# Turning attention and residual blocks by DMA instead of on TensorE, and the gate/up products in natural order of k

## The chip, the cores and the metric

One core of one Trainium2 chip runs the whole program. The metric is the device time of one execution in microseconds (us). The median of three runs of the kernel before is 2124.01 us.

## The reference, cut to what matters

A trunk of two pre-norm layers over a residual `h` of 256 positions by 2048 features, all in float32. Layer 0 mixes with sliding-window attention and an mLSTM, layer 1 with a forgetting attention (FoX) of 16 heads of 128. Each layer ends with a SwiGLU feed-forward of width 5632.

```python
for layer in range(DEPTH):
    xn = rms_norm(h, norm_mix[layer])
    mix = swa_mlstm_mixer(xn, ...) if layer % 2 == 0 else forgetting_attention_mixer(xn, ...)
    h = h + mix                                   # mix ends with "@ w_out"
    h = h + swiglu(rms_norm(h, norm_ffn[layer]), w_gate[layer], w_up[layer], w_down[layer])
return rms_norm(h, norm_final)

def forgetting_attention_mixer(xn, w_in, b_f, w_out):
    q, k, v, f = split_cols(xn @ w_in, FOX_SIZES)     # 16 heads of 128 for each of q, k, v
    s = q @ k.T * scale + c[:, None] - c[None, :]     # c: running sum of log sigmoid(f); causal
    return (softmax(s) @ v).reshape(B, S, FOX_MIX) @ w_out

def swiglu(xn, w_gate, w_up, w_down):
    return (silu(xn @ w_gate) * (xn @ w_up)) @ w_down
```

## The kernel before, in words

**A matrix product.** Every product with a weight matrix keeps float32 accuracy by splitting both factors into a rounded high part and a low rest, and adding three TensorE products (`hi*hi`, `hi*lo`, `lo*hi`). Weights come in chunks of 256 rows by 512 columns ("a k pair": two tiles of 128 rows). SyncE's DMA queue loads a chunk into `raw` (L105, 512 KB; four buffers in the pool `wr`), ScalarE casts it to `hi` (L161), VectorE subtracts to make `lo` (L162); `hi` and `lo` have six buffers each. The chunk is used by 12 matmuls of 512 columns, in `gemm` (L192 to L194) or in `pair_group` (through `three`, L402 to L404). The activations are the stationary operands and must have the features on the partitions: `xh`, `xl` hold the normed residual so turned and split, `mh`, `ml` the mixer's or the hidden result.

**Turning.** There are two ways to get a block turned. *On TensorE*: eight transposes of 128x128 through the identity into PSUM (L245 in `split_scaled` for the residual; L306 in `transpose_many`, followed by a VectorE copy at L307, for q and k). *By DMA*, in `split_turned`: ScalarE copies the block's float32 words apart into two planes of 16 bits (L272, two instructions), four `dma_start_transpose` on SyncE's queue turn the planes (L274), and later a function `join` puts the two halves of each word together again (L279, two ScalarE copies) and calls `split_scaled` on the result. `scrap` finds the two buffers for that. A block `n` of the residual is 512 features: k tiles 4n to 4n+3, so k pairs 2n and 2n+1.

**When a join runs.** `out_proj` and `ffn` put a join with a due step into a list (`later` or `todo`); `run_due` emits it right behind the chunk load of that step. In `gemm` the step is counted in chunks, in `pair_group` it is the position in the order of k pairs.

**The output projection** (`out_proj`) makes the four blocks of `h` in two halves, `n0` = 0 and 2. Blocks 0 and 1 are turned by DMA while the second half is computed; blocks 2 and 3 are turned on TensorE as soon as they are added.

**Gate and up** (`ffn` calls `pair_group` for each of 11 groups of 512 hidden features and each layer). Per group, eight k pairs of two matrices: the positions written `(0, pair)` in `ORDER` are plain (24 matmuls), those written `(1, pair)` are mixed (a Strassen-like form: 21 matmuls, but more VectorE operations, L440 to L443 and L295, and sums of the activations made by `sums_of`). Before, the mixed ones are pairs 2, 3 and 6 at positions 2, 4 and 6. The down projection uses the same function with its own orders `DOWN`, in which the mixed ones of a group of eight are pairs 1, 3 and 5 at positions 1, 3 and 5.

**FoX.** For each of four head groups `i`, q, k and v are projected in turn (16 k tiles each), q and k are scaled into a natural tile (L865 in `nat1`) and turned on TensorE into `qtf` and `ktf`, and the scores start after v (L316, L323).

**What sets the order.** The program is recorded as written; a scheduler then orders each engine's instructions ahead of time, and each engine and each DMA queue runs its own list strictly in order, held by semaphores. SyncE's list holds the chunk loads and the DMA transposes alike.

Of the kernel before, what the change touches and what calls it, by code (L numbers as in the profile page):

```python
# [7 lines left out]
F32 = mybir.dt.float32  # L8
# [24 lines left out]
OFF_QM, OFF_KM, OFF_VM, OFF_OM = 1536, 2048, 2560, 3584  # L33
CAP = 15.0
FILL = 24
ORDER = ((0, 0), (0, 1), (1, 2), (0, 4), (1, 3), (0, 5), (1, 6), (0, 7))
DOWN = {
    6: ((0, 0), (1, 1), (0, 2), (1, 3), (0, 4), (0, 5)),
    8: ((0, 0), (1, 1), (0, 2), (1, 3), (0, 4), (1, 5), (0, 6), (0, 7)),
}  # L40
MID = 6
MID_DOWN = 5
LATER = (6, 10)
LATER_DOWN = (5, 6)
RAWS = 4
PARTS = (0, 3, 7, 11)
# [9 lines left out]
def trunk(  # L56
# [153 lines left out]
    def square_sum(key, n):  # L210
        if n == 0:
            sums[key] = sm.tile([P, NT, 4], F32, tag="ss", name="ss")
        for t in range(NT):
            junk = sm.tile([P, NB], BF16, tag="junk", name="junk", bufs=1)
            nc.scalar.activation(
                junk, h[:, t, n * NB : (n + 1) * NB], AF.Square, accum_out=sums[key][:, t, n : n + 1]
            )
# [50 lines left out]
    def split_turned(idx, n, flat, turned, extra=None):  # L268
        planes = flat.bitcast(U16).rearrange("p (b t n) -> p b t n", b=2, t=NT)
        hu = h[:, :, n * NB : (n + 1) * NB].bitcast(U16).rearrange("p t (n b) -> p t n b", b=2)  # L270
        for b in range(2):
            nc.scalar.copy(planes[:, b, :, :], hu[:, :, :, b])  # L272
            for t in range(NT):
                nc.sync.dma_start_transpose(turned[:, b, :, t, :], planes[:, b, t, :])  # L274

        def join():
            ju = flat.bitcast(U16).rearrange("p (n b) -> p n b", b=2)
            for b in range(2):
                nc.scalar.copy(ju[:, :, b], turned[:, b, :, :, :].rearrange("p k t q -> p (k t q)"))  # L279
            split_scaled(idx, n, extra, flat.rearrange("p (k s) -> p k s", k=4))  # L280

        return join

    def scrap(fp, n):
        if n == 0:
            box = fp.tile([P, 4, NB], F32, tag="c", name="box", bufs=1)
            halves = box[:, 0:2, :], box[:, 2:4, :]
        else:
            halves = [fp.tile([P, CK, NB], F32, tag="raw", name="box", bufs=RAWS) for _ in range(2)]
        flat, turned = (a.rearrange("p a n -> p (a n)") for a in halves)  # L290
        return flat, turned.bitcast(U16).rearrange("p (b k t q) -> p b k t q", b=2, t=NT, q=P)
# [92 lines left out]
            split_plain(mh[:, ks, :], ml[:, ks, :], po)  # L384

    def out_proj(w, idx, key, extra):
        last = KT - 4
        for n0 in (0, 2):
            accs = [new_acc() for _ in range(2)]
            for i in range(2):  # L390
                gemm(accs[i], m_of, w, (n0 + i) * NB, NB, 0, last, KT, step=6 * i)
            for i in range(2):
                gemm(accs[i], m_of, w, (n0 + i) * NB, NB, last, KT, KT, step=6)
                add_out(accs[i], n0 + i)
                if n0 == 0:
                    later.append((LATER[i], split_turned(idx, i, *scrap(extra[2], i), extra)))
                else:
                    split_scaled(idx, n0 + i, extra)
                square_sum(key, n0 + i)

    def three(o, ah, al, hi, lo, start, stop):
        nc.tensor.matmul(o, ah, hi, start=start, stop=False)  # L402
# [67 lines left out]
        nc.vector.tensor_tensor(out=c[:, 3, :], in0=prods[1], in1=c[:, 1, :], op=ALU.add)  # L470
        return plain, c

    def ffn(layer, fp, sx, sd, key, idx_next=None, key_next=None, finish=None):
        r = rstd(key)

        def sums_x(pair):
# [3 lines left out]
        for g0, g1 in zip(PARTS, PARTS[1:]):  # L480
            end = g1 == PARTS[-1]
            nk = 4 * (g1 - g0)
            order = DOWN[nk // 2]
            todo = []
            for g in range(g0, g1):
                par = (g1 - 1 - g) % 2
                plain, c = pair_group(
# [99 lines left out]
    def close_layer(layer, w_out, idx, key, **rest):  # L587
        with tc.tile_pool(name=f"fp{layer}", bufs=2) as fp:
            nx = len(mixed_of(ORDER))
            nd = max(len(mixed_of(o)) for o in DOWN.values())  # L590
            sx = [fp.tile([P, nx, 4, P], F32R, name=f"sx{i}", bufs=1) for i in range(2)]
            sd = [fp.tile([P, nd, 4, P], F32R, name=f"sd{i}", bufs=1) for i in range(2)]
            out_proj(w_out, idx, key, (*sx, fp))
            ffn(layer, fp, sx, sd, key, **rest)


    acc0 = new_acc()
# [263 lines left out]
    with tc.tile_pool(name="od", bufs=1) as od:  # L861
        def nat1(acc, n, name, bufs=1):
            t_ = od.tile([P, NT, n], F32, tag=name, name=name, bufs=bufs)
            for t in range(NT):
                nc.scalar.mul(t_[:, t, :], acc[t][:, 0:n], r1[:, t : t + 1])  # L865
            return t_

        VT = 2 * FD
        c_v = 2 * FOX_H * FD
        acc = project(wi1, c_v + 14 * FD, VT + FOX_H)  # L870
        fg = od.tile([P, NT, FOX_H], F32, name="fg")
        for t in range(NT):
            nc.vector.scalar_tensor_tensor(
                out=fg[:, t, :],
                in0=acc[t][:, VT : VT + FOX_H],
                scalar=r1[:, t : t + 1],
                in1=bias_f,
                op0=ALU.mult,
                op1=ALU.add,
            )  # L880
        vtail = nat1(acc, VT, "vtail")
        nl = od.tile([P, NT, FOX_H], F32, name="nl")
        nc.scalar.activation(nl, fg, AF.Abs)
        nc.scalar.activation(nl, nl, AF.Exp, scale=-1.0)
        nc.scalar.activation(nl, nl, AF.Ln, bias=1.0)
        nc.vector.scalar_tensor_tensor(out=nl, in0=fg, scalar=0.0, in1=nl, op0=ALU.min, op1=ALU.subtract)
        nc.vector.tensor_scalar(nl, nl, -1.0, None, op0=ALU.mult)
        pc = pm.tile([P, NB], F32, tag="pm", name="pcf")
        nc.tensor.matmul(pc[:, 0:FOX_H], upper, nl[:, 0, :], start=True, stop=True)
        nc.tensor.matmul(pc[:, FOX_H : 2 * FOX_H], ones, nl[:, 0, :], start=True, stop=False)  # L890
        nc.tensor.matmul(pc[:, FOX_H : 2 * FOX_H], upper, nl[:, 1, :], start=False, stop=True)
        negc = od.tile([P, NT, FOX_H], F32, name="negc")
        nc.vector.tensor_copy(negc.rearrange("p t h -> p (t h)"), pc[:, 0 : 2 * FOX_H])
        pr = pm.tile([P, NB], F32, tag="pm", name="prf")
        nc.tensor.matmul(pr[0:FOX_H, 0:P], nl[:, 0, :], upper, start=True, stop=True)
        nc.tensor.matmul(pr[0:FOX_H, P:S], nl[:, 0, :], ones, start=True, stop=False)
        nc.tensor.matmul(pr[0:FOX_H, P:S], nl[:, 1, :], upper, start=False, stop=True)
        negct = od.tile([FOX_H, S], F32, name="negct")
        nc.vector.tensor_copy(negct, pr[0:FOX_H, 0:S])
        scratch = dp.tile([FOX_H, S], F32, name="scratch")  # L900
        nc.gpsimd.dma_start(scratch, negct)
        cb1 = od.tile([P, FOX_H, S], F32, name="cb1")
        nc.gpsimd.dma_start(cb1, scratch.partition_broadcast(P))
        cb0 = od.tile([P, FOX_H, P], F32, name="cb0")
        for dst, src in ((cb0, cb1[:, :, 0:P]), (cb1[:, :, P:S], cb1[:, :, P:S])):
            nc.gpsimd.affine_select(
                out=dst, in_=src, pattern=[[0, FOX_H], [-1, P]], compare_op=ALU.is_ge, fill=NEG, base=0, channel_multiplier=1
            )

        for i in range(4):  # L910
            qt = od.tile([P, 4, S], F32, tag="qt", name="qtf")
            kt = od.tile([P, 4, S], F32, tag="kt", name="ktf")
            for off, dst in ((0, qt), (FOX_H * FD, kt)):
                n_ = nat1(project(wi1, off + i * NB, NB), NB, "qk")
                for g in range(0, 4, 2):
                    transpose_many(
                        dst[:, g : g + 2, :].rearrange("p g (t q) -> p (g t) q", q=P),
                        [n_[:, t, (g + u) * FD : (g + u + 1) * FD] for u in range(2) for t in range(NT)],
                    )
            vn = nat1(project(wi1, c_v + i * NB, NB if i < 3 else VT), NB if i < 3 else VT, "vn")  # L920

            def v_of(j, b, i=i, vn=vn):
                if i == 3 and j >= 2:
                    return vtail[:, b, (j - 2) * FD : (j - 1) * FD]
                return vn[:, b, j * FD : (j + 1) * FD]

            attention(
                od,
                lambda j, b, qt=qt: qt[:, j, b * P : (b + 1) * P],
                lambda j, kt=kt: kt[:, j, :],  # L930
                v_of,
                FD,
                FD**-0.5,
                cb0[:, 4 * i : 4 * i + 4, :],
                cb1[:, 4 * i : 4 * i + 4, :],
                4 * i,
                negc=negc[:, :, 4 * i : 4 * i + 4],
            )
# [76 lines left out]
```

## Time and profile before

| | |
|---|---|
| median of three runs | 2124.01 us (2122.88 to 2124.37) |
| the profiled execution's own time | 2122.88 us |
| its span from first to last instruction | 2121.2 us, so 1.7 us lie around it |
| TensorE busy (PE) | 2105.2 us, 99% of the span |
| VectorE (DVE), ScalarE (ACT), GpSimd (POOL) busy | 1719.5, 1277.0, 39.6 us |
| granted TensorE clock | 0.999 |
| DMA engines, mean | 199 GB/s, 421.48 MB moved |

PE is the matmul, PEld its weight load; SPq is SyncE's DMA queue. A matmul's listed duration (389 ns) includes its time in the pipeline; the next one starts some 0.227 us later, and it is the distance from start to start that counts.

### The profile page before, as it was taken

To read this page: it belongs to the slowest core of one execution; us is meant where nothing else is said; L and a number is where in the kernel's file an instruction comes from. 1 tells how busy PE (TensorE), PEld (TensorE's weight loads), DVE (VectorE), ACT (ScalarE), POOL (GpSimd) and SP (SyncE) were. 2 spreads that over 40 slices of the span, in tenths; PEclk is the share of its full clock that TensorE was granted. 3 is DMA by queue.
4 is the path that set the end of the run, shared out by engine and by line. 5 is a ranking of instruction groups with operands and counts; after the bars stand their busy time and mean duration, and the time that the engine had idled before them with its cause. 6 is when DMAs were issued, how large, how long until landed. Compare 5 with 4: busy or idle time off the path is not lost.

```text
span 2121.2 us, 26858 instructions
## 1 busy us (share of the span) xinstructions
PE 2105.2 (99%) x9699; PEld 1747.9 (82%) x9699; DVE 1719.5 (81%) x2212; ACT 1277.0 (60%) x1612; POOL 39.6 (2%) x61
## 2 busy tenths in 40 slices
PE   8999999999999999999999999999999999999998
PEld 7888888888888888888888888888888888888886
DVE  6665558999999999999855554579999999989994
ACT  6565457765567656766645544576755667556763
POOL 2110000000000000000000000000000000000000
PEclk9999999999999999999999999999999999999999
DMA  8454547666567666666575564676656666656754
GB/s 267 145 157 149 170 149 268 209 203 215 191 211 225 215 207 216 209 202 215 163 231 168 169 179 140 194 237 210 215 196 208 218 196 224 225 188 212 224 182 147
DMA packets 267942, 421.48 MB, mean 199 GB/s; under 512 B 67136, under 2 KB 75424, under 8 KB 267552
## 3 DMA queue, kind: packets, MB, share of 16 engines
q1 hardware_dynamic: 267136, 416.02, 61.6%
q0 software_dynamic: 624, 3.72, 0.5%
q8 instruction: 76, 1.25, 0.2%
q14 instruction: 58, 0.48, 0.1%
q10 hardware_dynamic: 48, 0.02, 0.0%
HBM read 404.48 MB, written 2.11 MB: 192 GB/s over the span
## 4 chain that ended last, share of the span: by engine, by line
PE 98%; ACT 1%; issue 0%; DMA 0%; DVE 0%; DVEq 0%; POOLq 0%; POOL 0%; ACTq 0%
PE acc L402 17%; PE acc L403 17%; PE acc L404 17%; PE acc L192 10%; PE acc L193 10%; PE acc L194 10%; PE prod L402 4%; PE prod L403 4%; PE prod L404 4%; PE p L323 1%; PE ptm L306 1%; PE po L374 1%; PE pt L245 0%; PE pp L366 0%; PE p L316 0%
## 5 line engine op out<-in xcount | busy, mean ns | idle before, releaser
L161 ACT CAST hi<-raw 128x1024 fp32r<-128x1024 f32 (+2 forms) x681 | 692.5, 1032 | 598.5 <-PE acc L404 307.6
L162 DVE TENSOR_TENSOR lo<-raw,hi 128x1024 fp32r<-128x1024 f32 (+2 forms) x681 | 807.3, 1201 | 259.5 <-ACT hi L161 256.2
L403 PE MATMUL acc<-lo,xh 128*128 128x512 f32 x946 | 368.1, 389 | 0.0
L402 PE MATMUL acc<-hi,xh 128*128 128x512 f32 x946 | 367.4, 389 | 0.0
L404 PE MATMUL acc<-hi,xl 128*128 128x512 f32 x946 | 366.8, 389 | 0.0
L192 PE MATMUL acc<-hi,xh 128*128 128x512 f32 (+3 forms) x736 | 275.8, 377 | 0.8 <-ACT hi L161 0.8
L193 PE MATMUL acc<-lo,xh 128*128 128x512 f32 (+3 forms) x736 | 275.8, 375 | 0.0
L194 PE MATMUL acc<-hi,xl 128*128 128x512 f32 (+3 forms) x736 | 275.5, 376 | 0.0
L404 PEld LDWEIGHTS acc<-hi,xl 128*128 128x128 f32 x946 | 177.6, 188 | 36.9
L402 PEld LDWEIGHTS acc<-hi,xh 128*128 128x128 f32 x946 | 177.5, 188 | 36.8
L403 PEld LDWEIGHTS acc<-lo,xh 128*128 128x128 f32 x946 | 177.6, 188 | 36.7
L403 PE MATMUL acc<-lo,mh 128*128 128x512 f32 x437 | 170.0, 389 | 0.0
L402 PE MATMUL acc<-hi,mh 128*128 128x512 f32 x437 | 168.1, 389 | 0.0
L404 PE MATMUL acc<-hi,ml 128*128 128x512 f32 x437 | 167.9, 389 | 0.0
L192 PEld LDWEIGHTS acc<-hi,xh 128*128 128x128 f32 x736 | 138.7, 189 | 24.8 <-ACT hi L161 1.2
L193 PEld LDWEIGHTS acc<-lo,xh 128*128 128x128 f32 x736 | 139.0, 189 | 24.2 <-issue 0.9
L194 PEld LDWEIGHTS acc<-hi,xl 128*128 128x128 f32 x736 | 138.8, 189 | 24.5 <-issue 0.8
L295 DVE TENSOR_TENSOR lt<-raw,ht 128x1024 fp32r<-128x1024 f32 x95 | 115.9, 1220 | 15.6 <-ACT ht L294 15.6
L294 ACT CAST ht<-raw 128x1024 fp32r<-128x1024 f32 x95 | 99.8, 1050 | 45.7 <-PE acc L404 26.9
L192 PE MATMUL acc<-hi,mh 128*128 128x512 f32 x320 | 125.3, 392 | 1.2 <-ACT mh L294 1.2
L193 PE MATMUL acc<-lo,mh 128*128 128x512 f32 x320 | 125.3, 392 | 0.0
L194 PE MATMUL acc<-hi,ml 128*128 128x512 f32 x320 | 123.9, 390 | 0.0
(313 smaller groups left out, 3120.4 us busy)
## 6 DMA issues: line engine op xcount, KB each, us to landing
raw<-in_w_gate_dram SPq DMA_DIRECT2D x176, 512.0 KB, 4.4
raw<-in_w_up_dram SPq DMA_DIRECT2D x176, 512.0 KB, 4.7
raw<-in_w_down_dram SPq DMA_DIRECT2D x176, 512.0 KB, 4.8
raw<-in_w_in_odd_dram SPq DMA_DIRECT2D x88, 512.0 KB, 3.9
raw<-in_w_in_even_dram SPq DMA_DIRECT2D x64, 512.0 KB, 4.1
raw<-in_w_out_even_dram SPq DMA_DIRECT2D x32, 512.0 KB, 3.6
raw<-in_w_out_odd_dram SPq DMA_DIRECT2D x32, 512.0 KB, 4.1
raw<-in_w_in_odd_dram SPq DMA_DIRECT2D x8, 272.0 KB, 2.8
```

The costliest lines, as they stand in the source:

```text
L161: latest[0] = nc.scalar.copy(hi[:, :, 0:n], raw[:, :, 0:n])
L162: nc.vector.tensor_tensor(out=lo[:, :, 0:n], in0=raw[:, :, 0:n], in1=hi[:, :, 0:n].bitcast(F32), op=ALU.subtract)
L192: nc.tensor.matmul(o, ah[:, ts], hi, start=(k == 0), stop=False)
L193: nc.tensor.matmul(o, ah[:, ts], lo, start=False, stop=False)
L194: nc.tensor.matmul(o, al[:, ts], hi, start=False, stop=(k == k_all - 1))
L294: nc.scalar.copy(dst_h, src)
L295: nc.vector.tensor_tensor(out=dst_l, in0=src, in1=dst_h.bitcast(F32), op=ALU.subtract)
L306: nc.tensor.transpose(pt[:, i, :], s_, ident)
L323: nc.tensor.matmul(p1[:, jj, :], q_of(j, 1), k_of(j), start=True, stop=True)
L402: nc.tensor.matmul(o, ah, hi, start=start, stop=False)
L403: nc.tensor.matmul(o, ah, lo, start=False, stop=False)
L404: nc.tensor.matmul(o, al, hi, start=False, stop=stop)
```

## The change

`ORDER` now has the mixed pairs 1, 3 and 5 at positions 1, 3 and 5, with all pairs in natural order. Blocks 2 and 3 of both output projections are turned by DMA too; their joins are handed to the first gate/up group of the layer with due positions 3 and 5. `scrap` gives block 2 the buffer of `c`, block 3 that of the sums `sd0`, `sd1` (which are not used before the down projection). In FoX, q and k of head groups 0, 1 and 2 are turned by DMA in a new function `turn`, joined six chunks into the next projection; head group 3 stays on TensorE.

```diff
-ORDER = ((0, 0), (0, 1), (1, 2), (0, 4), (1, 3), (0, 5), (1, 6), (0, 7))
+ORDER = ((0, 0), (1, 1), (0, 2), (1, 3), (0, 4), (1, 5), (0, 6), (0, 7))
-LATER = (6, 10)
+AHEAD = 6
+LATER = (6, 10, 3, 5)
...
     def scrap(fp, n):
-        if n == 0:
+        if n % 2 == 0:
             box = fp.tile([P, 4, NB], F32, tag="c", name="box", bufs=1)
             halves = box[:, 0:2, :], box[:, 2:4, :]
+        elif n == 3:
+            halves = [fp.tile([P, 3, NB], F32, tag=f"sd{i}", name="box", bufs=1)[:, 0:CK, :] for i in range(2)]
         else:
             halves = [fp.tile([P, CK, NB], F32, tag="raw", name="box", bufs=RAWS) for _ in range(2)]
...
     def out_proj(w, idx, key, extra):
-        last = KT - 4
+        last, rest = KT - 4, []
...
-                if n0 == 0:
-                    later.append((LATER[i], split_turned(idx, i, *scrap(extra[2], i), extra)))
-                else:
-                    split_scaled(idx, n0 + i, extra)
+                (later if n0 == 0 else rest).append(
+                    (LATER[n0 + i], split_turned(idx, n0 + i, *scrap(extra[2], n0 + i), extra))
+                )
                 square_sum(key, n0 + i)
+        return rest
...
-    def ffn(layer, fp, sx, sd, key, idx_next=None, key_next=None, finish=None):
+    def ffn(layer, fp, sx, sd, key, todo, idx_next=None, key_next=None, finish=None):
...
-            todo = []
...
-            out_proj(w_out, idx, key, (*sx, fp))
-            ffn(layer, fp, sx, sd, key, **rest)
+            todo = out_proj(w_out, idx, key, (*sx, fp))
+            sd = [fp.tile([P, nd, 4, P], F32R, tag=f"sd{i}", name=f"sd{i}", bufs=1) for i in range(2)]
+            ffn(layer, fp, sx, sd, key, todo, **rest)
...
+        def turn(src, dst):
+            planes = od.tile([P, 2, NT, NB], U16, tag="planes", name="planes")
+            turned = od.tile([P, 2, 4, NT, P], U16, tag="turned", name="turned")
+            su = src.bitcast(U16).rearrange("p t (n b) -> p t n b", b=2)
+            for b in range(2):
+                nc.scalar.copy(planes[:, b, :, :], su[:, :, :, b])
+                for t in range(NT):
+                    nc.sync.dma_start_transpose(turned[:, b, :, t, :], planes[:, b, t, :])
+            def join():
+                du = dst.rearrange("p k s -> p (k s)").bitcast(U16).rearrange("p (n b) -> p n b", b=2)
+                for b in range(2):
+                    nc.scalar.copy(du[:, :, b], turned[:, b, :, :, :].rearrange("p k t q -> p (k t q)"))
+            return join
...
                 n_ = nat1(project(wi1, off + i * NB, NB), NB, "qk")
+                if i < 3:
+                    later.append((AHEAD, turn(n_, dst)))
+                    continue
```

More of the change, by code (lines that the diff above doesn't have):

```diff
@@ L591, in close_layer @@
             sx = [fp.tile([P, nx, 4, P], F32R, name=f"sx{i}", bufs=1) for i in range(2)]
-            sd = [fp.tile([P, nd, 4, P], F32R, name=f"sd{i}", bufs=1) for i in range(2)]
-            out_proj(w_out, idx, key, (*sx, fp))
-            ffn(layer, fp, sx, sd, key, **rest)
+            todo = out_proj(w_out, idx, key, (*sx, fp))
+            sd = [fp.tile([P, nd, 4, P], F32R, tag=f"sd{i}", name=f"sd{i}", bufs=1) for i in range(2)]
+            ffn(layer, fp, sx, sd, key, todo, **rest)
     acc0 = new_acc()
```

## The prediction

> **What bounds the kernel now.** I read the page first, then the waits of PE, then the chain where q is turned, then SyncE's queue, and last the busy time by stretches.
>
> The page: busy time, two rows of the 40 slices, the chain by engine.
>
> ```profile
> PE 2105.2 (99%) x9699; PEld 1747.9 (82%) x9699; DVE 1719.5 (81%) x2212; ACT 1277.0 (60%) x1612; POOL 39.6 (2%) x61
> PE   8999999999999999999999999999999999999998
> DVE  6665558999999999999855554579999999989994
> PE 98%; ACT 1%; issue 0%; DMA 0%; DVE 0%; DVEq 0%; POOLq 0%; POOL 0%; ACTq 0%
> ```
>
> All waits of PE in the whole program (waiting line, what ended it, us, times, longest):
>
> ```profile
> PE pg L146 <- DMA gn<-in_norm_mix_dram: 3.8, 1, 3.8
> PE pt L245 <- DMA h<-in_x_dram: 1.3, 1, 1.3
> PE acc L192 <- ACT mh L294: 1.2, 1, 1.2
> PE acc L192 <- ACT hi L161: 0.8, 1, 0.8
> PE pp L366 <- DVE s L358: 0.2, 1, 0.2
> ```
>
> They sum to 7.3 us, the first two at the start. PE is never kept waiting in a feed-forward or in FoX. So PE's instruction count is the time, and whatever leaves PE shortens the run, unless the engines that feed it fall behind. How near are they? VectorE is the one: over one gate/up group and one down group of eight (start:end, span, then PE, PEld, DVE, ACT busy)
>
> ```profile
> 579.00:620.00 41.00, 41.00 (x183) 33.96 (x182) 39.53 (x50) 28.24 (x31) 0.00 (x0) 1.00 0.69 218
> 703.00:745.00 42.00, 42.00 (x187) 34.77 (x186) 40.22 (x49) 27.03 (x29) 0.00 (x0) 1.00 0.63 203
> ```
>
> it is busy 96% in both, and ScalarE 69% and 64%. What protects PE is the lead of six `hi`/`lo` buffers. Pairing each `lo` or `lt` with the matmul that first reads it, the lead is 4 to 13 us in the feed-forwards (3.0 at its two smallest places, 509.7 and 1585.8), 1.4 where layer 1 begins at 1046, 7 at 1060, then 9 to 13 us through FoX and 6.0 near its end. One example, at the first gate/up group: VectorE's `lt` of the start 365.91 ends at 367.12, and its matmul starts at 371.89, a lead of 4.8.
>
> ```profile
> 365.91 1.21 DVE L295 TENSOR_TENSOR lt<-t,ht 128x1024 fp32r<-128x1024 f32 x1
> 371.89 0.39 PE L403 MATMUL prod<-lt,sx 128*128 128x512 f32 x1
> ```
>
> **What the change takes from PE.** A block is eight transposes. The q block of FoX's first head group in the chain (start, length, what):
>
> ```profile
> 1075.95 0.23 PE acc L192
> 1076.18 0.23 PE acc L193
> 1076.41 0.22 PE ptm L306 x2
> 1076.63 0.23 PE acc L194
> 1076.86 0.23 PE acc L192
> 1077.09 0.23 PE acc L193
> 1077.32 0.23 PE acc L194
> 1077.55 0.65 PE ptm L306 x6
> 1078.21 0.23 PE acc L192
> ```
>
> The two rows are 0.22 + 0.65 = 0.87 us; from 1075.95 to 1078.21 are 2.26 us, less six matmuls of 0.227 is 0.90. Both agree; I take 0.90. Ten blocks go: blocks 2 and 3 of two output projections (32 L245) and q, k of three head groups (48 L306). The number of weight matmuls stays: three mixed pairs of 21 and five plain of 24 per group, in either order. So PE loses 10 x 0.90 = **9.0 us**, 0.88 to 0.93 per block by where it is read.
>
> **What it adds elsewhere.** Per block: two copies into planes (L272, 1041 ns), four DMA transposes, two joining copies (L279, 1350 ns): 4.8 us of ScalarE, and SyncE's queue is held. Where eight were issued in a row:
>
> ```profile
> 304.11 10.45 SPq L274 DMA_TRANSPOSE box<-box  x8
> 314.66 2.06 SPq L105 DMA_DIRECT2D raw<-in_w_out_even_dram  x4
> ```
>
> 10.45 / 8 = 1.3 us each, against some 0.4 for a weight load, so a block holds back every weight load behind it by 5.2 us. There the next cast waited 3.3 us for its load, and the lead at 325 fell to 3.7 us without PE stopping.
>
> *FoX.* One head group takes 74 us, in which ScalarE is busy 36.0; two blocks make it 45.6, and VectorE loses four copies of 0.69 (L307). The held queue: a load goes out when the chunk four earlier has its `lo`, lands 3.9 us later (the page's median for this matrix), and is cast four chunks on, 4 x 2.72 = 10.9 us; the cover is 7.0 against 5.2, and behind that PE's lead of 9 to 13. The joins stand six of eight chunks into the next projection, so `ktf` is complete about two casts before the scores need it, with casts running five chunks (13 us) ahead of PE. I cost FoX at nothing; if the cover fell, one block would cost 5.2 less the lead, still nothing.
>
> *Order.* A group keeps its VectorE work. What moves is the first mixed pair: one plain pair (24 x 0.227 = 5.4 us) after the group's start instead of two. Its products go into the PSUM banks of the previous group's accumulators, so four additions (L494, 0.6 each apart) must be done in those 5.4 us; on the other side the products are free one pair earlier. The down groups of eight already run this very order at the same 96%, with four more additions at their end, and PE does not wait there. I cost it at nothing, with 0.4 us per group as the bound.
>
> *The handover to the feed-forward*, twice, is the tight place. Before, block 3 is added at 350.2 and turned by PE at 351 to 353. After, block 2 (added by 345.0): planes at 347, transposes to 352, landed 353.5, joined and scaled (2 x 1.25 + 4 x 0.41, from L279 and L252) by 359, needed at pair 4. Gate/up starts at 346.7; two plain and two mixed pairs later (2 x 5.44 + 2 x 4.76) that is 367, or 364 since the built order lets pair 4 start inside position 3. Block 3: planes by 351, landed 358, joined and scaled near 368, needed at pair 6 at 377, or 374 by the same overlap. Each block alone has 5 us to spare. ScalarE as a whole has not: from 344.3 to 373 it must do eight turning copies (8.8 us, at 0.95 and 1.25 from start to start), eight scalings (3.3), sums (1.3), four squares (2.5) and the casts of pairs 2 to 5 with the rest of pair 1 (11.5): 27.4 of 28.7 us, against 18.6 before. VectorE's work is only moved here, but it now has three mixed pairs done by position 5 instead of two, 4.6 us earlier. With the lead of 4 to 5 us I expect 0.5 us of waiting at each handover, with 0 and 3 as ends. Below zero is excluded: PE has no wait here to give back.
>
> **The sum**: 9.0 - 2 x 0.5 = 8.0 us. Of the profiled execution's 2122.9 that leaves 2114.9; the median of the runs is 1.1 higher, so **2116.0**.
>
> **A rule that speaks against it.** By the row, one transpose costs PE 0.11 us, and one DMA transpose (four to a block where PE needs eight) holds its queue 1.3 us. The Trainium skill ("VectorE: DVE Perf Modes", section "The three transpose paths") gives 390 ns on TensorE against 1309 ns by DMA, and advises TensorE wherever a PSUM result will do. By that rule the change goes the wrong way; it weighs the two alone, and the trace here has PE full and the queue not.
>
> **The rivals.**
>
> *Part of the gain goes back at the handover* (2118 to 2122). ScalarE's 27.4 of 28.7 us overflows, or block 3's transposes push the loads of positions 6 and 7 past their casts: 1.5 to 3.5 us per layer. For it: the margin above. Against: casts at 96% would still only eat the lead.
>
> *All of it goes back* (2120 to 2128): both handovers at 3 us or more and some lead missing in the next group, which regains only about 1.5 us per 41.5.
>
> *Slower through the new order.* The additions at L494 come late because VectorE is already in the next mixed pair, and the products' banks are not free: a wait of y per gate/up group, 22 times. It decides from y = 9.0 / 22 = 0.41 us on; at y = 0.8 the time is 2116 + 17.6 = 2134. For it: VectorE at 96% and the smallest leads (4.3 to 4.8) lie at the mixed pairs' `lt`. Against: the down groups.
>
> *Slower through the held queue.* If weight loads had no cover, ten blocks of 5.2 us were 52, less the 9.0: about 2167. The rule above is this rival's support; its condition, loads that land when the cast is due, shows in four or five casts per weight matrix (list of waits: some 5 us for each), while 307.6 us of ScalarE's waits for a cast are for a free buffer.
>
> That the change leaves the work on PE is excluded: the changed kernel's instruction lists have 80 transposes fewer on PE, 40 copies more on ScalarE, 40 DMA transposes more on SyncE and 12 copies fewer on VectorE.
>
> **How the numbers follow.** Forecast (2114 to 2118) 0.61; part given back 0.16, of which 0.12 ends below 2119.8; all given back 0.08; slower by order 0.12, by the queue 0.03. A difference under 0.2% (4.2 us) can't be told from none here. Faster: 0.61 + 0.12 = 0.73; same: 0.04 + 0.08 = 0.12; slower 0.15. Range: from the full 9.0 with 0.93 per block and a low run, 2113, to 2122.5, which holds the first two and a little of the third, 0.80.
>
> **What would show it.** Right: PE's list of waits unchanged after the start; the L245 group at x56 and the q, k one at x16; a span near 2113; SPq with 60 instead of 20 `box`-like transposes at 1.3 us; ScalarE near 1277 + 10 x 4.8 = 1325 busy. Wrong at the handover: PE waits on ACT `xh`, `ht` or `sx` around 360 to 380 and 1435 to 1455. Wrong on order: PE waits of L402 `prod` on DVE L494, 22 times. Wrong on the queue: ACT casts waiting for `raw` through FoX.

## The result and the profile after

The changed kernel takes 2114.07 us (median of five runs, 2113.45 to 2114.58) against 2124.01 us: ratio 0.9954, 95% interval 0.994 to 0.9969, so 9.9 us faster. The profiled execution took 2113.82 us with a span of 2112.1 us, 9.1 us less than before. Line numbers are one to three higher than before (L402 to L404 are now L405 to L407, L192 to L194 are L193 to L195, L245 is L246, L306 is L309, L274 is L275); in FoX, `turn` has its copies at L917, its transposes at L919 and its joins at L924.

The page of the changed kernel: busy time, the same two rows of slices, the chain by engine.

```profile
PE 2096.1 (99%) x9619; PEld 1740.3 (82%) x9619; DVE 1709.0 (81%) x2200; ACT 1315.5 (62%) x1652; POOL 38.7 (2%) x61
PE   8999999999999999999999999999999999999998
DVE  6665558999999999999845545579999999999994
PE 98%; ACT 1%; issue 0%; DMA 0%; DVE 0%; POOLq 0%; POOL 0%; DVEq 0%; ACTq 0%
```

PE has 80 instructions fewer and is busy 2105.2 - 2096.1 = 9.1 us less, which is the whole change of the span. The list of PE's waits (waiting line, what ended it, us in total, times, longest) is the old one with new line numbers, to the tenth:

```profile
PE pg L147 <- DMA gn<-in_norm_mix_dram: 3.8, 1, 3.8
PE pt L246 <- DMA h<-in_x_dram: 1.3, 1, 1.3
PE acc L193 <- ACT mh L297: 1.2, 1, 1.2
PE acc L193 <- ACT hi L162: 0.8, 1, 0.8
PE pp L369 <- DVE s L361: 0.2, 1, 0.2
```

Nothing that was added reaches PE. What moved is visible around it. The first gate/up group (the kernel before, then the changed one), then one of the later groups and a down group of the changed kernel (start:end, span, then PE, PEld, DVE, ACT, POOL busy with their counts, clock, DMA share, GB/s):

```profile
347.00:388.00 41.00, 41.00 (x190) 33.99 (x189) 38.89 (x55) 26.73 (x39) 0.69 (x1) 1.00 0.67 211
347.00:388.00 41.00, 41.00 (x182) 33.97 (x181) 38.31 (x54) 34.87 (x46) 0.69 (x1) 1.00 0.79 226
579.00:620.00 41.00, 41.00 (x183) 33.95 (x182) 39.61 (x51) 29.01 (x32) 0.00 (x0) 1.00 0.68 228
703.00:745.00 42.00, 42.00 (x187) 34.79 (x186) 40.36 (x50) 26.98 (x29) 0.00 (x0) 1.00 0.65 212
```

In the first group, ScalarE rose from 26.73 to 34.87 us. PE is full in both: 14 of its 190 instructions before were transposes at L245 of some 0.11 us each, and now longer matmuls fill the same 41 us, 182 in all. The other two rows stand as before: VectorE busy 97% and 96%, PE full. The new order of k pairs changes nothing in these two rows.

Where the time was gained shows when the same matmuls of the two traces are paired. At 345 us the changed kernel is 0.3 us late: it started 1.2 us earlier and lost 1.6 near 190 us, both outside the stages that were edited. Then it gains 1.9 us at the output projection of layer 0, 5.6 in FoX and 1.9 at the output projection of layer 1: 9.4 us, 0.94 for each of ten blocks. The 9.1 us of the spans are these 9.4 less the 0.3.

### The profile page after: what moved, and what is told of

It is laid out like the page before. It is cut to its first block, busy times and chain, and to the rows that moved or that the text cites. A ratio compares the mean times of both kernels' runs of the same rounds, so it can differ in the third digit from the quotient of the medians.

```text
span 2112.1 us, 26841 instructions
## 1 busy us (share of the span) xinstructions
PE 2096.1 (99%) x9619; PEld 1740.3 (82%) x9619; DVE 1709.0 (81%) x2200; ACT 1315.5 (62%) x1652; POOL 38.7 (2%) x61
## 4 chain that ended last, share of the span: by engine, by line
PE 98%; ACT 1%; issue 0%; DMA 0%; DVE 0%; POOLq 0%; POOL 0%; DVEq 0%; ACTq 0%
PE acc L405 17%; PE acc L407 17%; PE acc L406 17%; PE acc L193 11%; PE acc L194 10%; PE acc L195 10%; PE prod L405 4%; PE prod L407 4%; PE prod L406 4%; PE p L326 1%; PE po L377 1%; PE pp L369 0%; PE ptm L309 0%; PE p L319 0%; PE po L378 0%
## 5 line engine op out<-in xcount | busy, mean ns | idle before, releaser
L405 PE MATMUL acc<-hi,xh 128*128 128x512 f32 x946 | 367.3, 389 | 0.0
L407 PE MATMUL acc<-hi,xl 128*128 128x512 f32 x946 | 366.4, 389 | 0.0
L193 PE MATMUL acc<-hi,xh 128*128 128x512 f32 (+3 forms) x736 | 275.5, 377 | 0.8 <-ACT hi L162 0.8
L194 PE MATMUL acc<-lo,xh 128*128 128x512 f32 (+3 forms) x736 | 275.9, 375 | 0.0
L195 PE MATMUL acc<-hi,xl 128*128 128x512 f32 (+3 forms) x736 | 275.2, 376 | 0.0
L407 PEld LDWEIGHTS acc<-hi,xl 128*128 128x128 f32 x946 | 177.6, 188 | 36.9
L405 PEld LDWEIGHTS acc<-hi,xh 128*128 128x128 f32 x946 | 177.6, 188 | 36.8
L407 PE MATMUL acc<-hi,ml 128*128 128x512 f32 x437 | 168.4, 389 | 0.0
L405 PE MATMUL acc<-hi,mh 128*128 128x512 f32 x437 | 168.1, 389 | 0.0
L193 PEld LDWEIGHTS acc<-hi,xh 128*128 128x128 f32 x736 | 138.8, 189 | 25.2 <-ACT hi L162 1.2
L194 PEld LDWEIGHTS acc<-lo,xh 128*128 128x128 f32 x736 | 139.1, 189 | 24.4 <-issue 0.9
L195 PEld LDWEIGHTS acc<-hi,xl 128*128 128x128 f32 x736 | 138.9, 189 | 24.6 <-issue 0.8
L193 PE MATMUL acc<-hi,mh 128*128 128x512 f32 x320 | 125.2, 391 | 1.2 <-ACT mh L297 1.2
L194 PE MATMUL acc<-lo,mh 128*128 128x512 f32 x320 | 125.2, 392 | 0.0
L195 PE MATMUL acc<-hi,ml 128*128 128x512 f32 x320 | 123.9, 390 | 0.0
L297 ACT CAST hi<-raw 128x512 fp32r<-128x512 f32 x95 | 59.0, 621 | 98.5 <-PE acc L407 87.8
L298 DVE TENSOR_TENSOR lt<-t,ht 128x1024 fp32r<-128x1024 f32 x95 | 115.9, 1220 | 4.5 <-ACT ht L297 4.2
```

The source lines that it names most:

```text
L193: nc.tensor.matmul(o, ah[:, ts], hi, start=(k == 0), stop=False)
L194: nc.tensor.matmul(o, ah[:, ts], lo, start=False, stop=False)
L195: nc.tensor.matmul(o, al[:, ts], hi, start=False, stop=(k == k_all - 1))
L297: nc.scalar.copy(dst_h, src)
L298: nc.vector.tensor_tensor(out=dst_l, in0=src, in1=dst_h.bitcast(F32), op=ALU.subtract)
L407: nc.tensor.matmul(o, al, hi, start=False, stop=stop)
```

## The experiments

The kernel before, timed on the same chip beside each set of runs, had medians of 2123.69 us (the first four), 2123.4 (the next four), 2123.18 and 2123.42.

**FoX alone.** The kernel before with `turn` for head groups 0 to 2:

```diff
+                if i < 3:
+                    later.append((AHEAD, turn(n_, dst)))
+                    continue
```

> Only q and k of FoX head groups 0 to 2 are turned by DMA; output projections and order as before. Theory (TensorE's list is the time, the feeding engines have lead enough): six blocks of eight transposes leave TensorE, 6 x 0.90 = 5.4 us less, about 2118.6, no new wait of TensorE. Rival 1 (the held queue of SyncE costs something in FoX): less than 4 us gained, and TensorE waits for ACT hi between 1070 and 1290. Rival 2 (the gain comes from the output projections and the new order): no more than 2 us.

Measured: 2117.78 us (2116.93 to 2118.78), ratio 0.9972 (0.9961 to 0.9983), 5.9 us below the kernel before. PE's waits are unchanged. Pairing the same matmuls of the two traces, PE stands at -0.03 us ahead of the first of these blocks and at -1.87, -3.75 and -5.64 after each of the three head groups: 0.94 us per block, and nowhere is any of it given back.

**The output projections alone.** Blocks 2 and 3 by DMA with the new order, q and k as before:

```diff
-LATER = (6, 10)
+LATER = (6, 10, 3, 5)
...
+                (later if n0 == 0 else rest).append(
+                    (LATER[n0 + i], split_turned(idx, n0 + i, *scrap(extra[2], n0 + i), extra))
+                )
```

> Only blocks 2 and 3 of both output projections are turned by DMA, with the new order of k pairs; FoX as before. Theory: four blocks, 4 x 0.90 = 3.6 us less, about 2120.4, no new wait of TensorE. Rival (the handover eats part of it): 1 to 2.6 us less and waits of TensorE for ACT xh, ht or sx around 360 to 380 and 1435 to 1455.

Measured: 2119.81 us (2119.2 to 2120.55), 0.9982 (0.9973 to 0.9991), 3.9 us below before. No wait of PE at either handover. The two parts add up: 5.9 + 3.9 = 9.8 of the 9.9 us.

**The order alone.**

```diff
-ORDER = ((0, 0), (0, 1), (1, 2), (0, 4), (1, 3), (0, 5), (1, 6), (0, 7))
+ORDER = ((0, 0), (1, 1), (0, 2), (1, 3), (0, 4), (1, 5), (0, 6), (0, 7))
```

> Only the order of the k pairs is changed (mixed pairs 1, 3, 5 at positions 1, 3, 5); every turn stays as before. Theory: the same matmuls in another order and leads of over 3 us, so 0 us of difference, 2124 within 1.5. Rival (the order itself costs or brings something): slower by 0.4 us per gate/up group, 9 us, with waits of L402 prod on DVE; or some us faster.

Measured: 2124.99 us (2124.02 to 2125.31), 1.0006 (0.9997 to 1.0014): not told apart from no change. In its profile PE is already 1.2 us late at 195 us, before any gate and up matmul has run, and still 1.2 us late at 350; at the start of layer 1 and at its FoX the difference is 1.3. So the 22 groups of the new order cost nothing that a trace shows; the 1.2 us are 1.6 lost near 190 us less a start 0.4 us earlier, and the last section shows that place.

**The changed kernel with the old order.**

```diff
-ORDER = ((0, 0), (1, 1), (0, 2), (1, 3), (0, 4), (1, 5), (0, 6), (0, 7))
+ORDER = ((0, 0), (0, 1), (1, 2), (0, 4), (1, 3), (0, 5), (1, 6), (0, 7))
```

> All blocks turned by DMA as in the changed kernel, but gate and up keep the old order (mixed pairs 2, 3, 6 at positions 2, 4, 6), in which pair 4, the first of block 2, comes at position 3 instead of 4. Theory: block 2 was ready near 359 to 363 and pair 4 now starts 4.8 us earlier than in natural order, near 362, so TensorE waits 0 to 3 us at each handover: 2114 to 2120, a wait on ACT xh or DVE xl near 362 and 1437. Rival (the order doesn't matter at all): as the changed kernel, 2114, and no wait.

Measured: 2115.96 us (2115.63 to 2116.34), 0.9964 (0.9951 to 0.9976), 1.9 us above the changed kernel. One line is new among PE's waits:

```profile
PE acc L405 <- ACT mh L297: 1.0, 2, 0.5
```

It is not where it was expected: the two waits of 0.5 us lie at 489 and 1558, where the first down group of each layer takes the hidden result that ScalarE has just split, not at the handovers near 362 and 1437. There ScalarE casts weights first, and `mh` only at 489.27. Paired with the changed kernel, this one is 0.55 us late at 345 us, ahead of the order, 1.37 from 512 on and 2.13 from 1580 on, which is the difference of the spans (2114.2 and 2112.1 us). So each of the two waits costs 0.8 us, more than the 0.5 that is listed: the first of these matmuls starts 0.98 us after the one before it, where 0.23 is usual. The new order goes with the blocks: alone it gives nothing, with them it spares some 1.6 us.

**The last head group too.** In the changed kernel:

```diff
-                if i < 3:
+                if i < 4:
```

> The kernel after, with q and k of the last head group of layer 1 turned by DMA too (8 blocks there instead of 6, so 16 more transposes leave TensorE). Theory (TensorE is the bound, a block of 8 transposes is worth 0.92 to 0.94 us as in the runs so far, and nothing else is late): 1.9 us below the kernel after, some 2112.2 us (2111.6 to 2112.8), no new wait of TensorE. Rival (the last group has the narrower v, 256 columns instead of 512, so less TensorE work stands between its k block and its scores, and the joined block comes late): TensorE waits for ACT's join ahead of the last scores by 1 to 4 us, and the time is 2112.5 to 2116.

Measured: 2112.3 us (2111.2 to 2112.6), 0.9948 (0.9935 to 0.996), 1.8 us below the changed kernel, and no new wait: the theory. The narrower v shows only in a lead (from the end of a `lo` to the matmul that first reads it) of 4.2 us at its smallest after 1290 instead of 6.0.

**SyncE's queue held twice as long in FoX, and four times.** Each transpose of `turn` is issued again, once and three times, into a tile that is never read:

```diff
                     nc.sync.dma_start_transpose(turned[:, b, :, t, :], planes[:, b, t, :])
+                    for _ in range(1):          # range(3) in the second
+                        nc.sync.dma_start_transpose(spare[:, :, t, :], planes[:, b, t, :])
```

> The kernel after, with each DMA transpose of the six head-group blocks issued a second time into a tile that nobody reads: 8 issues of 1.3 us for a block instead of 4, so SyncE's queue is held 10.4 us instead of 5.2 ahead of the next weight loads. Theory (the loads stand far enough ahead: TensorE leads its weights by 8.6 to 12.7 us there, and ACT's casts first use up the raw buffers that are loaded): no new wait of TensorE, 2114.1 us (2113.4 to 2115). Rival (the cover is only as long as the 5.2 us that the change holds): TensorE waits 2 to 5 us for each of six blocks, 2126 to 2144 us.

Measured: 2114.8 us (2114.71 to 2114.93), 0.996 (0.9946 to 0.9974): the median is inside the theory's range, and 0.7 us above the changed kernel's. PE's list of waits has no new line, but one of its lines has grown from `0.2, 1, 0.2`:

```profile
PE pp L369 <- DVE s L361: 0.6, 2, 0.4
```

That is TensorE waiting for a softmax in the third head group. Paired with the changed kernel, PE loses 0.95 us there, between 1273 and 1276 us, and no more than 0.15 us anywhere else in FoX. And ScalarE waits for loads now. Its two largest waits in FoX (1066 to 1300 us), the changed kernel first:

```profile
ACT hi L162 <- PE acc L195: 59.5, 40, 3.8
ACT hi L162 <- DMA raw<-in_w_in_odd_dram: 10.7, 10, 3.3
```

and with twice the transposes:

```profile
ACT hi L162 <- DMA raw<-in_w_in_odd_dram: 39.4, 33, 3.9
ACT hi L162 <- PE acc L195: 16.8, 12, 2.6
```

The two rows have changed places: casts that used to wait for a free buffer (PE) wait for their load. PE's smallest lead between 1070 and 1290 us shows how much of the cover is used up: 9.1 us before, 8.6 with the change, 3.4 here. So the loads of the weights are still covered. What reached PE came by another path: the joins wait longer for their turned planes (12.8 us for q and 13.6 for k in all, against 4.1 for q alone in the changed kernel), and the VectorE step of the softmax that PE waits for (L361) starts at 1273.78 us instead of 1268.76.

> The same with three more issues for each transpose: 16 issues, SyncE's queue held about 21 us a block. Theory (cover of some 7 us by loaded raw buffers plus a lead of 8.6 to 12.7 us, 16 to 20 us together): now it shows, TensorE waits 1 to 5 us for ACT's casts of the weights behind each of six blocks, 2120 to 2144 us. Rival (the queue is not on the way to TensorE at all in this stage): 2114 us as after.

Measured: 2179.93 us (2178.79 to 2180.88), 1.0268 (1.0253 to 1.0284): the direction of the theory, with a size well beyond it, 66 us or 11 per block. The page's list of PE's waits begins with the line

```profile
PE acc L193 <- ACT hi L162: 51.0, 7, 12.0
```

of which one wait, 0.8 us, is the usual one at the start. The other six are at the blocks: 6.6, 11.6, 3.5, 12.0, 4.6 and 12.0 us, 3.5 to 6.6 behind a q block and some 12 behind a k block. The other 14 us are in PE's busy time (2110.2 us against 2096.1): after each wait the matmuls run at a lower granted clock. The stretch of such a wait and the one behind it, with the clock after the POOL column:

```profile
1094.00:1098.00 4.00, 0.82 (x4) 0.36 (x2) 0.00 (x0) 0.00 (x0) 0.00 (x0) 1.00 0.51 101
1098.00:1104.00 6.00, 2.55 (x5) 1.63 (x6) 2.45 (x2) 3.38 (x4) 0.00 (x0) 0.58 1.03 331
```

The joins take part: each waits for its planes on ScalarE, 29.8 us in six waits, with casts queued behind it.

**Block 1 between the layers by DMA too**, which the change leaves on TensorE:

```diff
-                    if n < 1:
+                    if n < 2:
                         todo.append((LATER_DOWN[n], split_turned(idx_next, n, *scrap(fp, n))))
```

> The kernel after, with block 1 between the layers turned by DMA as block 0 is already (8 more transposes leave TensorE; the joined halves are due at step 6 of the next projection). Theory: 0.9 us below the kernel after, 2113.1 us (2112.5 to 2113.8), no new wait. Rival (the block ends 2 steps nearer to its first use than block 0, and ACT has RMSNorm's work of the new layer to do): TensorE waits 0.5 to 3 us for the split of that block near 1010 to 1020 us, 2114.5 to 2117.

Measured: 2137.19 us (2136.69 to 2137.41), 1.0065 (1.0053 to 1.0078), 23 us slower than the changed kernel, a cost that neither side expected. SyncE's queue from 964 us on (start, length, what) in the changed kernel:

```profile
964.43 24.52 SPq L106 DMA_DIRECT2D raw<-in_w_down_dram  x13
993.46 5.13 SPq L275 DMA_TRANSPOSE box<-box  x4
998.68 5.15 SPq L106 DMA_DIRECT2D raw<-in_w_down_dram  x5
```

and with block 1 turned by DMA, followed by the longest of the queue's waits for ScalarE:

```profile
964.73 16.80 SPq L106 DMA_DIRECT2D raw<-in_w_down_dram  x8
990.73 10.35 SPq L275 DMA_TRANSPOSE box<-box  x8
1001.12 32.96 SPq L106 DMA_DIRECT2D raw<-in_w_down_dram  x10
...
SPq L275 <- ACT box L273: 10.8, 2, 10.1
```

In the changed kernel thirteen loads go out ahead of the transposes; here eight. The queue then stands for 10.1 us until ScalarE has the planes, with the loads of the next columns behind it. What differs besides the number of transposes is where the block lies meanwhile: `scrap` gives block 1 two of the four `raw` buffers that weights are loaded into.

**Block 1's box with one raw buffer instead of two**, its turned halves in two of the small `tmp` tiles:

```diff
+    def scrap_small(fp):
+        flat = fp.tile([P, CK, NB], F32, tag="raw", name="box", bufs=RAWS).rearrange("p a n -> p (a n)")
+        return flat, [fp.tile([P, 4, NT, P], U16, tag="tmp", name="turned") for _ in range(2)]
```

> The kernel of the run before with block 1 between the layers by DMA (2137.2 us), but its box takes one of the four raw buffers that the weights are loaded into, not two: the turned halves go to two of the small tmp tiles. Theory (its 23 us were the two raw buffers that its box held from 994 to 1047 us, so that ACT waited for weights): with one buffer held most of it goes, 2113 to 2120 us, and ACT's wait for raw<-in_w_down_dram falls from 24 us to under 8 us. Rival (they were the four transposes ahead of the loads on SyncE's queue, or the join's copies on ACT): it stays at 2134 to 2138 us.

Measured: 2131.08 us (2130.2 to 2131.95), 1.0038 (1.0025 to 1.0051). The theory as written fell: one buffer less gives back 6 of the 23 us, and ScalarE's waits for w_down are 19.2 us, not under 8. The queue is the same as with two: eight loads, eight transposes, and only then the loads.

**Block 3's box in raw buffers**, one part of the change undone:

```diff
-        elif n == 3:
-            halves = [fp.tile([P, 3, NB], F32, tag=f"sd{i}", name="box", bufs=1)[:, 0:CK, :] for i in range(2)]
```

> The kernel after with one part of the change undone: the box of block 3 of the output projection lies in two raw buffers, as block 1's does, and not under the name of the sd tiles. Theory (raw buffers are what loads wait for): two of the four are held from the end of the output projection to step 5 of the first gate and up group in each layer, TensorE waits for ACT's casts of the weights there, 8 to 23 us a layer, 2130 to 2160 us. Rival (buffers are no limit): 2114 us as after.

Measured: 2153.19 us (2152.71 to 2153.84), 1.0142 (1.0128 to 1.0156): 39 us slower than the changed kernel, 19.6 per handover, within what the theory gave. At 343 us the eight transposes of blocks 2 and 3 run in a row, and no gate or up load comes between them as the two at 350.69 and 351.31 do in the changed kernel. PE waits 7.0 us in two for ScalarE's casts in the first handover, with smaller waits behind.

**Two raw buffers held without a block.**

```diff
+                    if n == 1:
+                        held = [fp.tile([P, CK, NB], F32, tag="raw", name="held", bufs=RAWS) for _ in range(2)]
+                        for i in range(2):
+                            nc.gpsimd.memset(held[i][:, 0, 0:1], 0.0)
+                        todo.append((LATER_DOWN[n], lambda: nc.gpsimd.tensor_copy(held[0][:, 0, 1:2], held[1][:, 0, 0:1])))
```

> The kernel after with block 1 between the layers turned on TensorE as before; two raw buffers are taken at the place where that block's box would take them and given back at step 6 (one element of each written and read on GpSimd), no transpose and no copy added. Theory (the buffers alone made the 23 us): 2130 to 2138 us, TensorE waiting for ACT's casts between 990 and 1050 us. Rival (the transposes on SyncE's queue or the join on ACT made them): 2114 us as after.

Measured: 2113.76 us (2113.04 to 2114.11), 0.9956 (0.9941 to 0.9972), the rival's number, but the run tells nothing. GpSimd has nothing else to do there: it wrote the tiles at 959.0 and 963.5 and ran the releasing copy at 963.7, so the buffers were held for 5 us and not until step 6.

**Both remaining sets of blocks, block 1's box in the `sx` tiles**, which nobody reads after the last gate and up group:

```diff
-                if i < 3:
+                if i < 4:
...
+    def scrap(fp, n, free=None):
+        if free:
+            halves = [fp.tile([P, 3, NB], F32, tag=f"{free}{i}", name="box", bufs=1)[:, 0:CK, :] for i in range(2)]
...
+                    if n < 2:
+                        todo.append((LATER_DOWN[n], split_turned(idx_next, n, *scrap(fp, n, "sx" if n else None))))
```

> The kernel after with both further blocks turned by DMA that remain between the layers and in layer 1's head groups: q and k of the last head group, as in the run on group 3 (2112.3 us), and block 1 between the layers, whose box now lies in the sx tiles, which nobody reads once the last gate and up group is done, and not in the raw buffers of the weights. Theory (what cost 23 us in the run on that block was only that its box lay in raw buffers, which the loads of the next columns need, so that these loads stood behind its transposes on SyncE's queue): 0.9 us below 2112.3, 2111.4 us (2110.4 to 2112.2), and five loads of w_down ahead of the transposes again. Rival (the four more transposes or the join's copies on ACT were the cost): 2128 to 2136 us, with TensorE waiting for ACT's casts between 990 and 1050 us.

Measured: 2111.51 us (2111.12 to 2111.84), 0.9943 (0.993 to 0.9957): the theory's 2111.4, and faster than both kernels. SyncE's queue at the same place:

```profile
965.54 24.46 SPq L106 DMA_DIRECT2D raw<-in_w_down_dram  x13
993.96 5.12 SPq L275 DMA_TRANSPOSE box<-box  x4
999.18 0.53 SPq L106 DMA_DIRECT2D raw<-in_w_down_dram  x1
999.81 5.13 SPq L275 DMA_TRANSPOSE box<-box  x4
```

The same eight transposes and the same copies on ScalarE as in the 23 us run, but thirteen loads ahead again, and PE's waits are those of before. So the place of the box was the cost. Whether it acts by the buffers missing or by the loads that then stand behind the transposes is not separated; that the second matters is suggested by the run with one raw buffer, which had the same queue and most of the loss.

## Why the prediction was right, step by step

**PE is the bound, and a block's transposes leave it.** Right. The sum had 0.90 us a block; FoX alone gives 0.94 by the trace, and so does the changed kernel over all ten blocks. The rows that were named came out: 56 transposes at L246, 16 of q and k at L309, 60 DMA transposes at a median of 1.26 us (36 at L275, 24 at L919), a span of 2112.1 us.

**The handover** is the term that was mis-sized. It was put at 0.5 us of waiting each and measured 0: the list of PE's waits has no new line, in the changed kernel and with the output projections alone. The load on ScalarE was foreseen rightly: from 344.3 to 373 it is busy 28.63 of 28.7 us, where the prediction had 27.4 (before it was 21.01, where the prediction had 18.6). ScalarE had no free time left there, and still PE did not wait, because the smallest lead there fell only from 4.8 to 3.6 us. Both blocks came in time, though near: block 2's last scaling ended at 361.8 and its first matmul started at 364.7, block 3's at 372.9 and 374.2. It was the lead, not ScalarE's free time, that had to be used up before PE waits. Without this term the sum is 9.0 us and the forecast 2115.0 us, 0.9 from the measured median: 0.4 of that are the 0.04 us by which each of ten blocks was put too low, and the rest is less than the spread of the five runs (1.1 us).

**The order at nothing.** Right, by the run of the order alone: no wait of PE on VectorE's additions (L494, now L496), and PE's offset against the kernel before is the same ahead of and behind the groups to 0.2 us. Not foreseen: with the blocks moved, the old order would have cost some 1.6 us, and at the first down group, not at the handover.

**FoX at nothing, by cover and lead.** Right in the result, a little too generous in the cover. It was put at 7.0 us; the smallest lead fell by 0.5 us under a hold of 5.2, and by 5.7 us under 10.4, and both give an estimate of 4.7 us of cover. For the run with four times the transposes that would be 20.8 - 4.7 - 9.1 = 7.0 us of wait for each block. The six waits are 8.4 us in the mean, but 7.0 describes none of them: behind the q blocks they are 3.5 to 6.6, behind the k blocks some 12. A k block follows a held q block, and the joins wait too; the sum has neither, so the cover holds for one block by itself. The sign named for a wrong step, casts waiting for `raw` in FoX, did appear (10.7 us in ten waits, before one of 2.1) while PE lost nothing: it was the wrong sign, because the lead stands between a late cast and PE. Nor does the sum of cover and lead have the path by which the doubled hold first cost anything: late joins, then a late softmax.

**ScalarE's busy time** was put at 1325 and is 1315.5. The instructions did add 48 us (the sum of all their durations rose from 1360.9 to 1408.9), but the page counts overlapping stretches once, and copies in a row overlap: 1041 ns long, 950 from start to start.

**The rule that spoke against it.** The Trainium skill ("VectorE: DVE Perf Modes", section "The three transpose paths") gives 390 ns on TensorE and 1309 ns by DMA, both for a block of 128x128. The rows here are of another kind: a DMA transpose of 128x512 holds SyncE's queue for 1.26 us and lands some 2.5 us after its issue, and a transpose on PE takes 0.11 us from start to start. The advice to use TensorE wherever a PSUM result will do stands in another section of the same page of the Trainium skill, "Rules for kernel authors". It does not hold for this kernel: ten blocks away from TensorE are worth 9.9 us by the medians and 9.4 by the trace, because PE is the bound and SyncE's queue has cover.

**A rival that was near without being named.** Both sides treated the box as free. In raw buffers, block 3's box alone costs 39 us, four times the gain; the two lines in `scrap` that put it under `sd` decide the sign of the whole change.

## What to carry to other kernels

When one engine is busy 99% and almost never waits, an operation that moves off it is worth its start-to-start time, even if the new way is several times longer, as long as the leads cover it; measure the cover by the smallest lead before and after, not by busy shares or by who waits upstream. Pair the matmuls of the two traces as well: a loss can come by another path, as the late joins did, and a list of waits shows less than PE loses (0.5 us listed for 0.8 lost). Ask of a moved step also in which buffers its data lie meanwhile: if they are those of the prefetch, on a queue that runs in order, the loads fall in behind the step, and a gain of 1 us becomes a loss of 23. And a hold that is meant as an experiment has to be released by an engine that is really at that point of the program.

## What the hardware showed besides

A wait of PE is paid more than once: with SyncE's queue held for 20.8 us, 51 us of waits came with 14 us of slower matmuls, at granted clocks of 0.50 to 0.77 in the stretches behind them. The Trainium skill ("TensorE: Matmul & The Clock Gate", section "What's actually happening") says that the array drops to half its clock after an idle window of some 3.4 us and needs a busy one to come back. The rows agree with that: the six waits are 3.5 to 12.0 us long.

The granted clock also fell once without any wait of PE. In some of the profiles, the changed kernel's among them, it is 0.50 for about 3 us near 190 us; matmuls then start 0.43 instead of 0.23 us apart, and PE is 1.6 us later. The stretch in the changed kernel, then in the kernel before:

```profile
190.00:192.00 2.00, 2.00 (x6) 1.56 (x5) 0.59 (x1) 1.97 (x5) 0.00 (x0) 0.50 0.00 0
```

```profile
190.00:192.00 2.00, 2.00 (x11) 1.72 (x12) 1.82 (x6) 1.90 (x7) 0.00 (x0) 1.00 0.04 13
```

It lies in a stage that no edit touches. Eight of fourteen profiles have it (the order alone and the old order among them, FoX alone and the last head group not). The changed kernel has it and the run with the held buffers, whose program is the same up to there, has not, so it belongs to the execution and not to the kernel. It makes two spans differ by 1.6 us, a sixth of the effect studied here; stretches of the trace and medians are the safer comparison. In the changed kernel it begins behind 3.2 us in which PE is listed as busy but works on products with 4 partitions only (185.46 to 188.68, L728, L729 and L752, with two of L727 among them). The same section of the Trainium skill says that the window is free-running. That the same stretch would then fill a window in one execution and not in another is an inference, and no run here shows it; the cause of this drop stays open.
